# Two groups of the gMLP's down projection by Strassen's seven products, woven between its channel blocks

## The chip, the cores and the metric

The kernel runs on one core of one Trainium2 chip. The metric is the device time of one execution in microseconds (us), median over runs. The core has a matmul engine (PE, with its weight loads PEld), a vector engine (DVE), a scalar engine (ACT), GpSimd (POOL) and a sync engine (SP); each runs its own list of instructions in order, and they meet through semaphores. SP's list here is mostly weight loads from device memory; POOL's list holds some small operations and a few transfers.

## The reference, cut to what matters

Two layers, each FFN, mixer, FFN, gated embedding; the mixer of the first layer is an mLSTM, that of the second a gMLP. Everything is float32; x is 512 tokens by 1024 channels. The mixer in question:

```python
def gmlp_mixer(x, w_in, b_in, vn_g, vn_b, ws, bs, w_out):
    B, S, _ = x.shape
    NB = S // GM_BLOCK                                   # 4 blocks of 128 tokens
    u, v = jnp.split(jax.nn.gelu(x @ w_in + b_in, approximate=False), 2, axis=-1)   # 2048 channels each
    v = layer_norm(v, vn_g, vn_b).reshape(B, NB, GM_BLOCK, GM_GROUPS, GM_GDIM)
    blk = jnp.arange(GM_BLOCK) // CHUNK
    mask = blk[:, None] >= blk[None, :]
    ws_m = jnp.where(mask, ws, jnp.zeros((), ws.dtype))
    s = jnp.einsum('gts,bnsgc->bntgc', ws_m, v) + bs.T[:, :, None]
    return (u * s.reshape(B, S, GM_WIDTH)) @ w_out       # 512x2048 @ 2048x1024
```

The change is about the last line, the product with `w_out`.

## The kernel before, in words

**Precision.** Every float32 operand is split into a high and a low part (`split`: ACT makes the high part by a rounding copy, L273 for activations and L193 for weights; DVE subtracts it from the operand for the low part, L274 and L199). A product is then three matmuls, high by high, high by low, low by high: `mm3`, L268 to L270. For some weight tiles the low part is made by ACT and a DMA of POOL that adds the operand (L196, L197), which `release(low="dma")` asks for.

**Weights.** `Weights` holds one list (`order`) of all tiles of weights in the order in which they are used. A tile's raw operand comes from a load into one of three raw buffers (SP, L162); `fill` splits tiles into high and low ("main" buffers, four, and "extra" ones, two) as soon as `release` gives a buffer back, and each split frees, at its raw operand's last use, the raw buffer for the next load. So loads, ACT's and DVE's splits all follow from where `release` stands in the program. Loads go out in the order of the list.

**Strassen.** `Group` already does the FFNs' and the mLSTM's down projections by Strassen's seven products (Winograd's form) of two by two blocks: seven products where eight would do. Left factors come from `form` (additions on DVE, in place on the activations, then a split into `fhi`, `flo`), right factors from `Weights.forms` (additions on DVE, L105, L106, L110, L111, in place on the raw weights), products go to pinned PSUM banks `gps`, and `add` adds each product's bank to the residual `xt` (L591, L593).

**The gMLP.** After v has been normalised, the 2048 channels go by in 16 blocks of 128. In step b of the loop at the end of `gmlp`: `spatial(b)` is eight small matmuls into two banks `sps`, and DVE's five operations that make s from them (`gadd`, `gs`); `split_v(b+2)` splits the v of a later block (`gvh`, `gvl`, `gv`); `gate_u(b+1)` projects the next block's u with 24 matmuls into a bank `gups`, and ACT applies the Gelu (`guf`, L1280); `gated` multiplies s by u (L1315) and splits it into `hh`, `hl`; then one `release`. After the steps 3, 7, 11 and 15, `down` does four blocks at once: 96 matmuls into banks `dps`, added to `xt` by DVE. `up_bank` cycles over four PSUM banks, which `gups` and most `sps` share, so that a matmul into a bank waits for the bank's last reader: DVE's `gs` or ACT's `guf`.

Of the kernel before, what the change touches and what calls it, by code (L numbers as in the profile page):

```python
# [16 lines left out]
P = 128  # L17
# [3 lines left out]
TB = SEQ // P  # L21
# [216 lines left out]
def hybrid_trunk(ctx: ExitStack, tc, x, p, ln_g, ln_b, ffn1_wgu, ffn1_wd, ffn2_wgu, ffn2_wd,  # L238
# [9 lines left out]
    def stage_pool(name, bufs=1):  # L248
        return tc.tile_pool(name=name, bufs=bufs, side="left", reuse_waits="tile")
# [16 lines left out]
    def mm3(ps, st, mv, start, stop, more=False):  # L266

        mm(ps, st[0], mv[0], start=start, stop=False, skip_group_check=more)  # L268
        mm(ps, st[0], mv[1], start=False, stop=False, skip_group_check=more)  # L269
        mm(ps, st[1], mv[0], start=False, stop=stop, skip_group_check=more)  # L270
# [38 lines left out]
    def kp(w):  # L309
        return w.rearrange("(kb p) c -> p kb c", p=P)  # L310
# [56 lines left out]

    ML_SLOTS = (2, 3, 4, 5, 6, 7, 11)

    def stage_kinds(first):  # L370

        n = len(W.order) - first
        for i in range(n):
            extra = i % 6 >= 4 if i < n // 6 * 6 else i >= n - 2
            W.order[first + i] = ("extra" if extra else "main",) + W.order[first + i][1:]

    def ml_weights():
        win, wout = ml_w_in[0], ml_w_out[0]
        first = len(W.order)
        for h in range(HEADS):  # L380
            at = len(W.order)
            W.add((w_cols(win, h * DQK), cols2))
            W.add((w_cols(win, QK + h * DQK), cols2))
            add_wide(win, 2 * QK + h * DV)
            z0 = 2 * QK + INNER + h * DV
            W.add((w_cols(win, z0), cols2))
            W.add((w_cols(win, z0 + 2 * P), cols2))
            if h:
                tiles = W.order[at:]
                del W.order[at:]  # L390
                k = 4 * h - 4
                j0, j1 = W.add_load(kp(wout)[:, k:k + 2, :], 3), W.add_load(kp(wout)[:, k + 2:k + 4, :], 3, "gb")
                left, right = ((slice(None), slice(None), slice(c, c + 512)) for c in (0, 512))
                down_w = W.forms("", (j0, left), (j0, right), (j1, right), (j1, left))
                for i, tile_i in enumerate(tiles):
                    W.order.append(tile_i)
                    if i in ML_SLOTS:
                        W.order.append(down_w[ML_SLOTS.index(i)])
        add_rows(wout, 4 * HEADS - 4, 4)
        stage_kinds(first)  # L400
        for i, kind in zip(range(-4, 0), ("main", "extra", "extra", "main")):
            W.order[i] = (kind,) + W.order[i][1:]

    def gm_weights():
        win, wout = gm_w_in[0], gm_w_out[0]
        first = len(W.order)
        for c in range(4):
            add_wide(win, GW + c * 512)
        for b in range(16):
# [4 lines left out]
            if b and b % 4 == 0:  # L414
                add_rows(wout, b - 4, 4)
        add_rows(wout, 12, 4)
        stage_kinds(first)
# [312 lines left out]
    class Group:  # L730
# [2 lines left out]

        TO = ((0, 0), (0, 0), (0, 1), (1, 1), (1, 1), (0, 1), (1, 0))

        def __init__(self, h, pool, first=False):
            self.h, self.pool, self.half = h, pool, h.shape[1] // 2

            self.first = (0, 2, 3, 6) if first else ()
            self.ready, self.banks = deque(), []  # L740
            self.next_form = self.next_product = self.next_add = 0

        def form(self):

            def a(i, j):
                m = self.half
                return self.h[:, m * j - m:m * j, (i - 1) * 256:i * 256]
            a11, a12, a21, a22 = a(1, 1), a(1, 2), a(2, 1), a(2, 2)
            r = self.next_form
            if r == 7:  # L750
                return
            self.next_form += 1
            if r == 2:
                vec.tensor_add(a21, a21, a22)
                vec.tensor_sub(a11, a21, a11)  # L755
            elif r == 4:
                vec.tensor_sub(a21, a22, a11)
# [442 lines left out]


    def gmlp():
        with stage_pool("extra", EXTRA) as extra, stage_pool("gm_parts") as near, stage_pool("ghpool", 4) as hpool, \
                stage_pool("gm") as mp:
            W.open("extra", extra, EXTRA)
            vf = mp.tile([P, TB, GW], F32, name="gvf")

# [103 lines left out]
                    vs.append(split_v(b + 2))  # L1311
                return s

            def gated(s, uf):
                vec.tensor_mul(s, s, uf)  # L1315
                h = new_h(hpool)
                split(h[0], h[1], s)
                return h

            vs = deque([split_v(0), split_v(1)])  # L1320
            us, ss, hs = deque(), deque(), []
            for b in range(2):
                us.append(gate_u(b))
            for b in range(16):
                if b in (0, 14):
                    ss.extend(spatial(i, vs.popleft()) for i in (b, b + 1))
                    if b == 0:

                        W.refill(2)
                        W.release(2, low="dma")  # L1330
                elif b not in (1, 15):
                    ss.append(spatial(b, vs.popleft()))
                ahead = 0 < b < 15
                if ahead:
                    us.append(gate_u(b + 1))
                hs.append(gated(ss.popleft(), us.popleft()))
                if ahead and b < 14:
                    W.release(low="dma")
                elif b == 15:
                    W.release()  # L1340
                if b % 4 == 3:
                    down(hs, b == 3, Norm(1, 1) if b == 15 else None)
                    hs = []
            W.close("extra")

# [148 lines left out]
```

## Time and profile before

| | |
|---|---|
| median of 3 runs | 2232.38 us (2232.21 to 2232.38) |
| the profiled execution: its time, its span | 2232.51 us, 2230.8 us |
| PE, DVE, ACT busy, share of the span | 100%, 68%, 41% |
| PE's matmul rows in the program, before and with the change | 10173, 10149 |
| mean of one 128x512 matmul as listed | 389 ns |
| the gMLP's loop over blocks in this execution | about 1630 to 1812 us from the start |

In the profile each row names the line, the engine, the operation, what is written and read, and how often. Matmuls overlap in the array, so that the listed mean of one is its latency; the pace of a run of matmuls is read from the starts. Rows of waits give, for an engine, what ended its idle time, the sum, the count and the longest. The window view gives the busy time of each engine in a stretch of the span.

### The profile page before, as it was taken

Reading aid. Unit: us, or ns where it says so; the run is one execution under the profiler, and the core shown is the slowest. Engines: PE = TensorE matmul, PEld = TensorE weight load, DVE = VectorE, ACT = ScalarE, POOL = GpSimd, SP = SyncE. Lnnn points to the kernel's source line nnn. Section 1 sums busy time; section 2 is a strip of 40 time slices with the busy share of each in tenths; the row PEclk is TensorE's granted clock in tenths of the full one; section 3 lists DMA queues with packets and bytes.
Section 4 is the critical chain, followed back from the end, with each engine's and each line's share of the span. In section 5 each row is a group of like instructions: output and inputs, shape, how many; then the busy total and the mean of one; then the engine's idle time right before and its main releaser. Section 6 shows DMA issues by size and latency. Waiting matters only on the chain.

```text
span 2230.8 us, 26548 instructions
## 1 busy us (share of the span) xinstructions
PE 2220.3 (100%) x10589; PEld 1864.0 (84%) x10589; DVE 1526.0 (68%) x2240; ACT 913.9 (41%) x1298; POOL 101.8 (5%) x135
## 2 busy tenths in 40 slices
PE   9999999999999999999999999999999999999998
PEld 8888888888888888888889888888888888888887
DVE  5666667777776786666687666666666578666677
ACT  4333336454646533333255333334343453333332
POOL 1000000111101100000000000000010100000000
PEclk9999999999999999999999999999999999999999
DMA  7422323466847443332233422223355443332221
GB/s 231 130 93 88 95 85 100 100 149 135 166 107 161 123 139 126 95 104 67 95 123 122 133 86 87 93 87 109 106 142 142 104 151 123 122 113 85 85 85 57
DMA packets 202723, 253.56 MB, mean 114 GB/s; under 512 B 5812, under 2 KB 156468, under 8 KB 202600
## 3 DMA queue, kind: packets, MB, share of 16 engines
q1 hardware_dynamic: 168080, 211.83, 29.5%
q0 software_dynamic: 27904, 25.35, 7.9%
q10 hardware_dynamic: 6616, 14.69, 2.0%
q8 instruction: 83, 1.36, 0.2%
q14 instruction: 40, 0.33, 0.0%
HBM read 224.58 MB, written 2.11 MB: 102 GB/s over the span
## 4 chain that ended last, share of the span: by engine, by line
PE 99%; ACT 1%; DVE 0%; issue 0%; DVEq 0%; POOL 0%; POOLq 0%
PE fps L269 13%; PE fps L270 13%; PE fps L268 13%; PE gps L270 7%; PE gps L269 7%; PE gps L268 7%; PE dps L269 3%; PE dps L268 3%; PE dps L270 3%; PE gups L268 1%; PE vps L268 1%; PE zps L268 1%; PE zps L270 1%; PE vps L270 1%; PE gvps L268 1%; PE gups L269 1%
## 5 line engine op out<-in xcount | busy, mean ns | idle before, releaser
L268 PE MATMUL fps<-xh,whi 128*128 128x512 f32 x1312 | 510.7, 389 | 0.0
L269 PE MATMUL fps<-xl,whi 128*128 128x512 f32 x1312 | 510.5, 389 | 0.0
L270 PE MATMUL fps<-xh,wlo 128*128 128x512 f32 x1312 | 510.4, 389 | 0.0
L199 DVE TENSOR_TENSOR wlo<-wraw,whi 128x1024 fp32r<-128x1024 f32 (+1 forms) x286 | 345.4, 1218 | 149.5 <-ACT whi L193 147.8
L193 ACT ACTIVATE whi<-wraw 128x1024 fp32r<-128x1024 f32 (+1 forms) x334 | 346.5, 1048 | 185.8 <-PE fps L269 81.6
L199 DVE TENSOR_TENSOR wlo<-wquarter,whi 128x1024 fp32r<-128x1024 f32 (+1 forms) x140 | 156.5, 1118 | 218.2 <-ACT whi L193 218.2
L268 PEld LDWEIGHTS fps<-xh,whi 128*128 128x128 f32 x1312 | 246.3, 188 | 51.2
L269 PEld LDWEIGHTS fps<-xl,whi 128*128 128x128 f32 x1312 | 246.3, 188 | 51.1
L270 PEld LDWEIGHTS fps<-xh,wlo 128*128 128x128 f32 x1312 | 246.2, 188 | 51.0
L193 ACT ACTIVATE whi<-wquarter 128x1024 fp32r<-128x1024 f32 (+1 forms) x140 | 136.3, 974 | 279.8 <-PE gps L270 209.0
L270 PE MATMUL gps<-whi,flo 128*128 128x512 f32 x588 | 229.3, 390 | 0.0
L268 PE MATMUL gps<-whi,fhi 128*128 128x512 f32 x588 | 229.3, 390 | 0.0
L269 PE MATMUL gps<-wlo,fhi 128*128 128x512 f32 x588 | 229.2, 390 | 0.0
L593 DVE TENSOR_TENSOR xt<-xt,gps 128x512 f32<-128x512 f32 x282 | 180.3, 680 | 0.5 <-PE gps L270 0.5
L817 ACT ACTIVATE sg<-fps 128x512 f32<-128x512 f32 x80 | 47.9, 598 | 228.4 <-PE fps L270 228.4
L273 ACT ACTIVATE fhi<-h 128x512 fp32r<-128x512 f32 (+1 forms) x140 | 80.5, 581 | 142.9 <-DVE h L755 54.4
L269 PEld LDWEIGHTS gps<-wlo,fhi 128*128 128x128 f32 x588 | 110.4, 188 | 23.5
L268 PEld LDWEIGHTS gps<-whi,fhi 128*128 128x128 f32 x588 | 110.4, 188 | 23.3
L270 PEld LDWEIGHTS gps<-whi,flo 128*128 128x128 f32 x588 | 110.4, 188 | 23.3
L274 DVE TENSOR_TENSOR flo<-h,fhi 128x512 fp32r<-128x512 f32 (+1 forms) x140 | 87.2, 634 | 42.9 <-ACT fhi L273 42.9
L563 POOL TENSOR_TENSOR rs<-rs,eps_pow 128x1 f32<-128x1 f32 x32 | 20.6, 643 | 1556.4 <-DVE rs L562 1556.4
L466 ACT ACTIVATE xf<-xps,cols 128x128 f32<-128x128 f32 x160 | 59.8, 453 | 52.5 <-PE xps L461 52.5
(289 smaller groups left out, 3736.4 us busy)
## 6 DMA issues: line engine op xcount, KB each, us to landing
wraw<-in_ffn_wgu_dram SPq DMA_DIRECT2D x79, 1024.0 KB, 6.0
wquarter<-in_ffn_wd_dram SPq DMA_DIRECT2D x64, 512.0 KB, 3.7
wraw<-in_ml_w_in_dram SPq DMA_DIRECT2D x24, 1024.0 KB, 5.5
wlo<-wraw POOLq DMA_DIRECT2D x48, 512.0 KB, 6.5
wraw<-in_gm_w_in_dram SPq DMA_DIRECT2D x15, 1024.0 KB, 5.7
wraw<-in_ffn_wgu_dram SPq DMA_DIRECT2D x17, 512.0 KB, 4.0
wraw<-in_ffn_wd_dram SPq DMA_DIRECT2D x8, 1024.0 KB, 4.9
wraw<-in_ml_w_out_dram SPq DMA_DIRECT2D x8, 1024.0 KB, 4.9
```

Of the source, the lines that this page charges most:

```text
L193: self.nc.scalar.activation(hi[:, s], src[:, s], AF.Copy)
L199: self.nc.vector.tensor_sub(lo[:, s], src[:, s], hi[:, s].bitcast(F32))
L268: mm(ps, st[0], mv[0], start=start, stop=False, skip_group_check=more)
L269: mm(ps, st[0], mv[1], start=False, stop=False, skip_group_check=more)
L270: mm(ps, st[1], mv[0], start=False, stop=stop, skip_group_check=more)
L273: sca.activation(hi, src, AF.Copy)
L274: vec.tensor_sub(lo, src, hi.bitcast(F32))
L466: sca.activation(xf[:, k], ps[:, k], AF.Identity, scale=col("ln_g", norm.at + 4 * g + k), bias=col("ln_b", norm.at + 4 * g + k))
L563: pool.tensor_tensor(rs[:, 1:2], rs[:, 0:1], eps_pow, op=OP.pow)
L593: vec.tensor_add(dst, dst, ps)
L817: sca.activation(sg, ps, AF.Silu)
```

## The change: what it does

The blocks 0 to 3 and 4 to 7 are two groups; each goes down by `Group`'s seven products of 12 matmuls (84) in place of `down`'s 96. Blocks 8 to 15 still go by `down`, in two times four. The flag `by_tokens` only turns the layout of `Group`'s blocks. What moves with it:

- For blocks 0 to 7 the product s times u is written in place into `gvf` in float32, unsplit; DVE's additions of `form` work on it there, and each of seven factors is split, so the `hh`, `hl` of these blocks fall away.
- The table `GM_STEPS` says how many products stand behind each block: the first product behind block 3, one or two behind each until the last behind block 11. After each product DVE's addition of the product before last to `xt`, the next left factor (`form`), and then `release` follow.
- The two raw loads of a group's `w_out` (two rows of blocks each) and the seven right factors stand in `order` where their products come; eight DVE additions in all (four per group) are made in the raw weights, and the low parts of these seven tiles are made by DVE (L199) and not by ACT and POOL. A raw buffer that holds them is kept until the last factor.
- Loads of `gm_w_in` and `gm_w_out` alternate one by one in SP's list; before they went in pairs.
- `ghpool` has two buffers and not four; blocks 10, 11, 14 and 15 use the buffers of the left factors, and the splits of blocks 10 and 11 come behind the `release` of the weights.
- `stage_kinds` and `two_row_forms` are the rearranged code around it; the list of the mLSTM's weights stays the same.

```diff
+    GM_GROUPS = 2
+    GM_STEPS = {3: 1, 4: 1, 5: 2, 6: 2, 7: 2, 8: 1, 9: 2, 10: 2, 11: 1}
...
+    def two_row_forms(w, kind="raw"):
+        j0, j1 = W.add_load(w[:, :2], 3), W.add_load(w[:, 2:], 3, kind)
+        left, right = ((slice(None), slice(None), slice(c, c + 512)) for c in (0, 512))
+        return W.forms("", (j0, left), (j0, right), (j1, right), (j1, left))
...
+        down_w, k = deque(), 0
+        for b, tile_b in enumerate(tiles):
+            W.order.append(tile_b)
+            for _ in range(GM_STEPS.get(b - 1, 0)):
+                if not down_w:
+                    down_w.extend(two_row_forms(kp(wout)[:, k:k + 4, :]))
+                    k += 4
+                W.order.append(down_w.popleft())
+            if b % 4 == 0 and b > 4 * GM_GROUPS:
+                assert not down_w
                 add_rows(wout, b - 4, 4)
...
                 for k in range(self.half):
-                    mm3(ps, [a[:, k, e * P:(e + 1) * P] for a in f], [a[:, k] for a in w],
+                    i, j = (e, k) if self.by_tokens else (k, e)
+                    mm3(ps, [a[:, i, j * P:(j + 1) * P] for a in f], [a[:, k] for a in w],
                         k == 0 and r in (0, 1, 3), k == self.half - 1, r not in (0, 1, 3))
...
-            def gated(s, uf):
+            def gated(b, s, uf):
+                if b < 4 * GM_GROUPS:
+                    dst = vf[:, :, b * P:(b + 1) * P]
+                    vec.tensor_mul(dst, s.rearrange("p (t c) -> p t c", t=TB), uf.rearrange("p (t c) -> p t c", t=TB))
+                    return
                 vec.tensor_mul(s, s, uf)
...
             for b in range(16):
+                add()
...
-                hs.append(gated(ss.popleft(), us.popleft()))
-                if ahead and b < 14:
+                s = gated(b, ss.popleft(), us.popleft())
+                late = b >= 4 * GM_GROUPS and b % 4 >= 2 and b in GM_STEPS
+                if b >= 4 * GM_GROUPS and not late:
+                    split_gated(b, s)
+                if b in (2, 3):
+                    form()
+                for i in range(GM_STEPS.get(b, 0)):
+                    add()
+                    products.popleft().product()
+                    form()
+                    W.release(1 if i + 1 < GM_STEPS[b] else 2, low="dma")
+                if late:
+                    split_gated(b, s)
```

**Where instructions move: DVE at the start of the loop.** DVE's list in step 0, before: the low parts of two weight tiles, then the first gated products with their splits.

```order
L274 TENSOR_TENSOR gv<-gvf,gv 128x512
L199 TENSOR_TENSOR wlo<-wraw,whi 128x1024 x2
L1315 TENSOR_TENSOR gs<-gs,guf 128x512
L274 TENSOR_TENSOR hl<-gs,hh 128x512
L1315 TENSOR_TENSOR gs<-gs,guf 128x512
```

With the change (`wraw_12751` holds u weights, `wraw_12810` the first and `wraw_13042` the second half of the first group's `w_out`):

```order
L199 TENSOR_TENSOR wlo_13039<-wraw_12751,whi_13038 128x1024
L199 TENSOR_TENSOR wlo_13045<-wraw_12810,whi_13044 128x1024
L199 TENSOR_TENSOR wlo_13054<-wraw_13042,whi_13053 128x1024
L1344 TENSOR_TENSOR gvf_12285<-gs_13008,guf_12967 128x4x128
L1344 TENSOR_TENSOR gvf_12285<-gs_13029,guf_12994 128x4x128
L1329 SCALAR_TENSOR_TENSOR gadd_13103<-rsum_12616,cols_108 128x128
```

A third low part, of the tile that comes from `wraw_13042`, now stands ahead of the first gated products; that load is the one that reuses the buffer of `wraw_12751`.

**ACT between the Gelus of blocks 4 and 5.** Before, with `guf_13205` the Gelu of block 4 and `guf_13397` that of block 5 (the four whole tiles belong to `down` behind block 3):

```order
L1280 ACTIVATE guf_13205<-gups_13180,cols_108 128x512
L273 ACTIVATE hh_13208<-gs_13171 128x512
L193 ACTIVATE whi_13212<-wraw_13039 128x1024
L196 ACTIVATE wlo_13213<-wraw_13039 128x1024
L193 ACTIVATE whi_13311<-wraw_13050 128x1024
L193 ACTIVATE whi_13321<-wraw_13050 128x1024
L193 ACTIVATE whi_13333<-wraw_13099 128x1024
L193 ACTIVATE whi_13343<-wraw_13099 128x1024
L273 ACTIVATE gvh_13368<-gvf_12282 128x512
L1280 ACTIVATE guf_13397<-gups_13372,cols_108 128x512
```

With the change `guf_13198` is block 4's and `guf_13284` block 5's:

```order
L1306 ACTIVATE guf_13198<-gups_13173,cols_108 128x512
L273 ACTIVATE fhi_13201<-gvf_12285 128x512
L273 ACTIVATE fhi_13221<-gvf_12285 128x512
L193 ACTIVATE whi_13227<-wraw_12810 128x1024
L193 ACTIVATE whi_13231<-wraw_13091 128x1024
L196 ACTIVATE wlo_13232<-wraw_13091 128x1024
L273 ACTIVATE gvh_13255<-gvf_12285 128x512
L1306 ACTIVATE guf_13284<-gups_13259,cols_108 128x512
```

`whi_13227` reads the weights that DVE's L111 has just written in place, `fhi_13221` the activations that its L780 has written; both stand ahead of block 5's Gelu. The second bank of block 5's `sps` is the bank `gups_13259`.

**DVE behind block 7**, where the last product of the first group and the first of the second stand together; all of it is new there, in this order:

```order
L274 TENSOR_TENSOR flo<-gvf,fhi 128x512
L105 TENSOR_TENSOR wraw<-wraw 128x2x512
L106 TENSOR_TENSOR wraw<-wraw 128x2x512
L199 TENSOR_TENSOR wlo<-wraw,whi 128x1024
L613 SCALAR_TENSOR_TENSOR xt<-xt,gps 128x512 x2
L779 TENSOR_TENSOR gvf<-gvf 128x2x256
L780 TENSOR_TENSOR gvf<-gvf 128x2x256
L274 TENSOR_TENSOR flo<-gvf,fhi 128x512
L110 TENSOR_TENSOR wraw<-wraw 128x2x512
L111 TENSOR_TENSOR wraw<-wraw 128x2x512
L199 TENSOR_TENSOR wlo<-wraw,whi 128x1024
L615 TENSOR_TENSOR xt<-xt,gps 128x512 x2
```

Both pairs of weight additions of the second group and two left factors now come between the gated product of block 7 and the `gadd` of block 8; before, DVE had only the additions of `down`'s banks and low parts of weights there.

More of the change, by code (lines that the diff above doesn't have):

```diff
@@ L408, in gm_weights @@
             add_wide(win, GW + c * 512)
+        at = len(W.order)
         for b in range(16):
@@ L1312, in spatial, with split_gated, form, add @@
                 return s
-            def gated(s, uf):
-                vec.tensor_mul(s, s, uf)
-                h = new_h(hpool)
-                split(h[0], h[1], s)
-                return h
+            def gated(b, s, uf):
[3 more added lines that the diff above has]
+                    return
+                vec.tensor_mul(s, s, uf)
+                return s
+            def split_gated(b, s):
+                if b % 4 < 2:
+                    h = new_h(hpool)
+                else:
+                    h = [fpool.tile([P, 2, 256], F32R, name=n, tag=n).rearrange("p t c -> p (t c)") for n in ("fhi", "flo")]
+                split(h[0], h[1], s)
+                hs.append(h)
+            groups = [Group(vf[:, :, g * 512:(g + 1) * 512], fpool, g == 0, True) for g in range(GM_GROUPS)]
+            forms, products, added = (deque(g for g in groups for _ in range(7)) for _ in range(3))
+            def form():
+                if forms:
+                    forms.popleft().form()
+            def add():
+                if len(added) > len(products):
+                    added.popleft().add()
             vs = deque([split_v(0), split_v(1)])
```

29 lines of the change are left out of this document (16 added, 13 removed).

## The prediction

> **What bounds the kernel now.** First I read the page's busy time with its chain of waits, then PE's waits by releaser.
>
> ```profile
> PE 2220.3 (100%) x10589; PEld 1864.0 (84%) x10589; DVE 1526.0 (68%) x2240; ACT 913.9 (41%) x1298; POOL 101.8 (5%) x135
> PE 99%; ACT 1%; DVE 0%; issue 0%; DVEq 0%; POOL 0%; POOLq 0%
> PE warm L1447 <- POOL ident masks.py:199: 1.4, 1, 1.4
> PE sup L696 <- DVE wlo L199: 0.2, 1, 0.2
> PE sup L696 <- ACT whi L193: 0.2, 1, 0.2
> ```
>
> PE sets the end by itself: in 2230.8 us it waits three times, 1.8 us in all, at the start. So whatever PE is spared comes off the time, and whatever wait is put on it goes on in full. Next, windows of the gMLP loop (busy us and count of each engine), one of the mLSTM behind them for comparison:
>
> ```profile
> 1672.00:1720.00 48.00, 48.00 (x229) 40.30 (x228) 26.82 (x45) 19.57 (x25) 4.84 (x4) 1.00 0.57 132
> 1720.00:1767.00 47.00, 47.00 (x225) 39.45 (x224) 26.02 (x44) 18.56 (x24) 4.83 (x4) 1.00 0.57 123
> 530.00:630.00 100.00, 100.00 (x489) 84.30 (x488) 71.55 (x141) 52.66 (x76) 14.46 (x17) 1.00 0.63 137
> ```
>
> The columns are PE, PEld, DVE, ACT, POOL, the granted clock, DMA share and GB/s. In the gMLP DVE is busy 56% of PE's time (26.82 of 48.00), so there is room; the mLSTM, which already weaves such products in, has DVE at 72% and PE without a wait.
>
> **What is removed: 24 matmuls.** PE's timeline, start and latency:
>
> ```profile
> 1639.60 0.28 PE L1300 MATMUL sps<-wsp,gvh 128*128 128x256 f32 x1
> 1640.47 0.45 PE L268 MATMUL gups<-xh,whi 128*128 128x512 f32 x1
> 1645.98 0.28 PE L1300 MATMUL sps<-wsp,gv 128*128 128x256 f32 x1
> 1646.85 0.45 PE L268 MATMUL gups<-xh,whi 128*128 128x512 f32 x1
> ```
>
> 24 matmuls take 1645.98 - 1640.47 = 5.51 us, 0.23 each (the listed 389 ns is latency); eight `sps` take 0.87; a block step without products is 6.38. A product of 12 is then 2.75 us, and a group spares 12 of them. **Gain: 24 x 0.23 = 5.5 us.** The 24 matmuls are removed where PE is the only bound, so this is certain.
>
> **What is added on DVE.** Groups of DVE's instructions in the loop, and the two kinds of additions as the mLSTM and FFN have them:
>
> ```profile
> L199 DVE TENSOR_TENSOR wlo<-wraw,whi 128x1024 fp32r<-128x1024 f32 x15 | 18.3, 1224 | 6.9 <-ACT whi L193 6.0
> L593 DVE TENSOR_TENSOR xt<-xt,dps 128x512 f32<-128x512 f32 x22 | 14.8, 683 | 22.1 <-PE dps L270 22.1
> L1309 DVE SCALAR_TENSOR_TENSOR gs<-sps,cols,gs 128x256 f32<-128x256 f32 x28 | 13.6, 484 | 1.0
> L1307 DVE SCALAR_TENSOR_TENSOR gs<-sps,cols,gadd 128x256 f32<-128x256 f32 x28 | 13.4, 479 | 1.5
> L274 DVE TENSOR_TENSOR hl<-gs,hh 128x512 fp32r<-128x512 f32 x16 | 11.1, 693 | 22.3 <-ACT hh L273 22.3
> L1315 DVE TENSOR_TENSOR gs<-gs,guf 128x512 f32<-128x512 f32 x16 | 11.0, 685 | 0.0
> L1303 DVE SCALAR_TENSOR_TENSOR gadd<-rsum,cols 128x128 f32<-128x128 f32 x14 | 4.8, 345 | 0.0
> L274 DVE TENSOR_TENSOR gvl<-gvf,gvh 128x512 fp32r<-128x512 f32 x6 | 4.1, 681 | 0.0
> L105 DVE TENSOR_TENSOR wraw<-wraw x3: 1218/1219/1220, 464.9 to 660.5; 128x1024 f32<-128x1024 f32 x3
> L111 DVE TENSOR_TENSOR wraw<-wraw x3: 1226/1227/1227, 474.5 to 670.0; 128x1024 f32<-128x1024 f32 x3
> L757 DVE TENSOR_TENSOR h<-h x20: 418/684/685, 58.3 to 2106.2; 128x512 f32<-128x512 f32 x16, 128x256 f32<-128x256 f32 x4
> ```
>
> For one group of four blocks: 14 additions to `xt` at 0.68 (9.6), four additions of left factors at 0.68 (2.7), seven low parts `flo` at 0.69 (4.9), four additions of weights at 1.22 (4.9), seven `wlo` at 1.22 (8.6), and four times a block's own 0.35 + 4 x 0.48 + 0.68 + 0.69 = 3.64 (14.6): **45.3 us**. PE needs 4 x 6.38 + 7 x 2.75 = **44.8 us** for it. DVE goes from 56% to 101% before it waits for anything. And it does wait:
>
> ```profile
> DVE hl L274 <- ACT hh L273: 22.3, 16, 2.2
> DVE wlo L199 <- ACT whi L193: 6.0, 6, 1.8
> ACT whi L193 <- DVE wraw L111: 7.3, 2, 3.7
> L193 ACT ACTIVATE whi<-wraw 128x1024 fp32r<-128x1024 f32 x27 | 28.5, 1054 | 46.6 <-PE dps L270 46.6
> L196 ACT ACTIVATE wlo<-wraw 128x1024 fp32r<-128x1024 f32 x14 | 14.6, 1045 | 0.0
> L1280 ACT ACTIVATE guf<-gups,cols 128x512 f32<-128x512 f32 x14 | 9.6, 687 | 38.9 <-PE gups L270 38.9
> ```
>
> Each split that follows its operand at once holds DVE some 0.7 us for a `fhi` or `hh` and 1.1 for a `whi`: 7 x 0.7 + 2 x 1.1 = 7 us a group. The products do stretch over nine blocks, so that single steps are lighter; what decides is the order in which ACT and DVE stand in each other's way.
>
> **The first stall.** DVE's and SP's timelines where the loop begins, and the landing times (shortest, median, longest) of SP's loads in the loop, the page's lines of both kinds of load and of POOL's transfers, and two neighbours of ACT's timeline:
>
> ```profile
> 1638.22 2.35 DVE L199 TENSOR_TENSOR wlo<-wraw,whi 128x1024 fp32r<-128x1024 f32 x2
> 1640.49 0.68 DVE L1315 TENSOR_TENSOR gs<-gs,guf 128x512 f32<-128x512 f32 x1
> 1639.46 6.46 SPq L162 DMA_DIRECT2D wraw<-in_gm_w_in_dram  x2
> wraw<-in_gm_w_out_dram SPq DMA_DIRECT2D x8, 1024.0 KB, 4.9
> DMA to landing us min/median/max: 3.7/5.0/9.9
> wraw<-in_gm_w_in_dram SPq DMA_DIRECT2D x15, 1024.0 KB, 5.7
> wlo<-wraw POOLq DMA_DIRECT2D x48, 512.0 KB, 6.5
> 1648.61 1.05 ACT L193 ACTIVATE whi<-wraw 128x1024 fp32r<-128x1024 f32 x1
> 1649.56 1.04 ACT L196 ACTIVATE wlo<-wraw 128x1024 fp32r<-128x1024 f32 x1
> ```
>
> The load that goes out at 1639.46, when the first of those two `wlo` frees its buffer, is with the change the second half of `w_out`. By the median it lands at 1644.4; DVE's third `wlo`, which now stands ahead of the gated products, starts at 1645.5 behind its `whi`. DVE, free at 1640.6 before, has lost 4.9 us. From there I add the rows in DVE's order: third `wlo` and two gated products to 1648.0; block 2's `gadd`, `gs`, `gvl`, gated product 1651.5; `flo` of the first product 1652.1 (PE asks for it at 1652.4: in time); L105, L106 1654.6; `wlo` behind its `whi` 1656.9; block 3 and its gated product 1660.4; `flo` 1661.7; L779, L780 and the next `flo` 1664.4; L110, L111 **1666.8**. ACT, whose next in line is the `whi` of these weights, then does `whi`, `whi`, `wlo`, `gvh`, `guf`; neighbours start 0.95 apart where one is listed at 1.05, so these five take 4.2 from there: block 5's Gelu ends at **1671.0**. PE, without a wait until there, has block 4's projection from 1646.85, a product, `sps`, block 5's projection and a product behind it: 1646.85 + 5.51 + 2.75 + 0.87 + 5.51 + 2.75 + 0.44 = 1664.7, when it needs the bank that this Gelu reads. **Stall 6.4 us**; everything behind it in PE's queue waits along. With the load landing at 3.7 it is 5.2, at 9.9 it is 11.4; if two of DVE's waits for ACT are hidden by work in between, 4. Another 0.4 follows at block 6's projection, whose bank DVE's `gs` of block 4 still reads.
>
> **The second stall.** From 1671.5 PE goes on to block 9. The weights of block 9's u come from a load that waits for its buffer until POOL's transfer of block 8's low part, which ACT's `wlo` lets out near 1685, has landed 6.5 later; the load lands 5.7 after that, at 1697.5, and ACT's `whi` of it, first in its queue, holds the next `fhi` and block 8's Gelu. DVE then has a `flo`, a `wlo`, two additions, block 7's `gadd` and `gs`, `gv` and gated product, 1700.2 to 1706.5 by the rows above. Behind block 7 1.4 (`flo`), 2.4 (L105, L106), 2.3 (`wlo` behind `whi`), 1.3 (additions), 1.3 (L779, L780), 1.4 (`flo`) and 2.4 (L110, L111) follow on each other in ACT's and DVE's queues, with a wait of about 1 for a product among them: L111 ends near 1720, block 9's Gelu five instructions later at **1724.2**. PE, at two products a step, is there at 1717.2, after 1.0 of waiting for DVE's addition to a product's bank. **Stall 7.0 + 1.0**, 0.4 behind it; 4.6 with transfers as short as the shortest, 12 with one of 9.9.
>
> **Behind it.** For blocks 8 to 11 I come to 2.6 us of waits (the last products' additions 2.0, the late splits of block 11 0.6). That far down, gaps of DVE may have absorbed them: between 0 and 2.6 I take the middle, 1.3.
>
> **Free of cost:** the in-place gated product has L1315's size; fewer transfers by POOL only lighten its queue; two `hh` buffers are enough because blocks 0 to 7 use none, and if not, the wait would stand with the third term.
>
> **Sum:** 6.4 + 0.4 + 1.0 + 7.0 + 0.4 + 1.3 - 5.5 = +11.0 us. Against the profiled execution's 2232.5: 2243.5; the median of the runs is 0.1 lower, so **2243.4 us**. Its own bounds: 4.0 + 4.6 - 5.5 = +3.1 (2235.5) up to, say, one transfer at 9.9: +5 (2248.5).
>
> **Rivals.**
>
> *The clock falls in the stalls.* The row that speaks for it stands at the very start, where PE came from idleness:
>
> ```profile
> 1.43 3.67 PE L1447 MATMUL warm<-ident 128*128 128x128 f32 x16 [1.43 <-POOL ident masks.py:199]
> 7.64 1.25 PE L1447 MATMUL warm<-ident 128*128 128x128 f32 x10
> ```
>
> The same matmul takes 0.23 us at first and 0.125 after, so 16 of them lost 3.67 - 16 x 0.125 = 1.67 us, although the granted clock reads 1.00 in every window. If a stall of 6 us puts PE back into that state, both cost 1.7 more: 2246.8. Against it: no row shows PE idle for more than 1.4 us later on. [...]
>
> *The stalls are hidden.* What decides is ACT's place: if block 5's Gelu ended by 1664.7, 6.4 us earlier than I have it, nothing would wait. For it: in the mLSTM L111 holds ACT 3.7 us at a time and PE never waits; DVE's lateness starts with one load, and the splits may overlap better than one behind the other. Then only the gain is left: 2232.4 - 5.5 = 2226.9, **faster**. Against it: 101% of DVE's time.
>
> *One stall alone.* If the early load lands soon and DVE catches up in the light steps, one stall of about 5 to 7 eats the gain: 2232 to 2234, the same.
>
> **How the numbers follow.** Forecast 0.50, clock rival 0.20, hidden 0.17, one stall 0.13. Over 0.2% (4.5 us, about what a measurement of this kernel can tell) lies all of the first two but the forecast's lowest end: slower 0.70; same 0.13; faster 0.17. The likeliest's own range is 2235.5 to 2248.5. The range reaches up to 2250 for the clock rival and down to 2226.5 to take in the hidden case, since leaving that out would leave out 0.17 and the upper tail.
>
> **What would show it.** PE's waits name `sps <- ACT guf` twice, near 1664 and 1717, of 4 to 8 us; DVE above 90% between 1645 and 1720; DVE's third `wlo` idle some 5 us for ACT's `whi`; the load of `w_out` issued at 1639.5. PE's matmuls 24 fewer at 0.23. I am wrong if PE waits for under 5.5 us in the loop, or if it waits for weights (`gups <- POOL wlo`) and not for banks.

## The result: 0.75% slower, from two stalls and what follows them

| | before | after |
|---|---|---|
| median | 2232.35 us (2232.21 to 2232.38, 4 runs) | 2249.07 us (2248.78 to 2249.48, 4 runs) |
| profiled execution: time, span | 2232.51, 2230.8 us | 2248.95, 2247.2 us |

The ratio is 1.0075, 95% interval 1.0058 to 1.0093: +16.7 us, where +11.0 was forecast. The page of the changed kernel, busy time and the chain that ended last:

```profile
PE 2221.3 (99%) x10565; PEld 1862.5 (83%) x10565; DVE 1555.4 (69%) x2279; ACT 923.9 (41%) x1311; POOL 105.7 (5%) x136
...
PE 95%; DVE 2%; ACT 1%; DMA 1%; issue 1%; SPq 0%; DVEq 0%; ACTq 0%; POOLq 0%
```

24 matmuls fewer (10565 are listed, 10589 before), and yet PE is listed as busy 1.0 us longer, in a span 16.4 us longer. The chain now runs 5% of the way through other engines, where it was 1%. PE's waits by releaser (sum, times, longest):

```profile
PE sps L1326 <- ACT guf L1306: 12.4, 2, 6.3
...
PE dps L268 <- DVE xt L615: 1.2, 1, 1.2
PE dps L268 <- ACT fhi L273: 0.7, 1, 0.7
```

Two waits for the bank that a Gelu reads, and two short ones at the end of the woven stretch: 14.3 us. Where they lie, and what else happens there, the windows of 10 us show (PE, PEld, DVE, ACT, POOL, granted clock, DMA share, GB/s):

```profile
1650.00:1660.00 10.00, 10.00 (x49) 8.26 (x48) 8.63 (x15) 2.64 (x4) 0.71 (x1) 1.00 0.77 144
1660.00:1670.00 10.00, 5.63 (x25) 4.02 (x23) 7.33 (x9) 3.47 (x5) 0.00 (x0) 0.94 0.04 13
1670.00:1680.00 10.00, 8.11 (x30) 6.79 (x31) 9.68 (x18) 4.95 (x8) 1.54 (x1) 0.72 0.69 129
...
1710.00:1720.00 10.00, 8.39 (x40) 6.86 (x38) 7.99 (x10) 1.69 (x2) 0.00 (x0) 1.00 0.39 112
1720.00:1730.00 10.00, 5.47 (x15) 4.51 (x16) 7.82 (x14) 6.57 (x9) 1.54 (x1) 0.67 0.47 52
```

PE loses 4.37 + 1.89 us in the first place and 1.61 + 4.53 in the second. But where it is busy again, it does less: from 1670 to 1680 it gets 30 matmuls done in 8.11 us, where 49 go into a full window. The granted clock there is 0.72, behind the second stall 0.67, and 1.00 in the windows where nothing waits. PE's timeline behind the first stall shows the pace:

```profile
1671.89 0.58 PE L1326 MATMUL sps<-wsp,gv 128*128 128x256 f32 x1 [6.26 <-ACT guf L1306]
...
1672.83 0.77 PE L268 MATMUL gups<-xh,whi 128*128 128x512 f32 x1
...
1674.67 0.63 PE L269 MATMUL gups<-xl,whi 128*128 128x512 f32 x1
1675.10 0.60 PE L270 MATMUL gups<-xh,wlo 128*128 128x512 f32 x1
1675.53 0.40 PE L268 MATMUL gups<-xh,whi 128*128 128x512 f32 x1
1675.77 0.39 PE L269 MATMUL gups<-xl,whi 128*128 128x512 f32 x1
```

Matmuls of one shape start 0.43 us apart until 1675.5 and 0.23 apart from there. Behind the second stall (it ends at 1724.53, after 6.14 us) the slow pace lasts until 1730.2. By the starts, against 0.23 for a matmul, the slow ones lose 1.7 and 2.7 us.

Now the chain of events that was forecast for the first stall, from SP's, ACT's and DVE's timelines of the changed kernel:

```profile
1639.51 0.37 SPq L162 DMA_DIRECT2D wraw<-in_gm_w_out_dram  x1
...
1645.34 1.06 ACT L193 ACTIVATE whi<-wraw 128x1024 fp32r<-128x1024 f32 x1 [6.63 <-DMA wraw<-in_gm_w_out_dram]
1646.43 1.23 DVE L199 TENSOR_TENSOR wlo<-wraw,whi 128x1024 fp32r<-128x1024 f32 x1 [5.82 <-ACT whi L193]
...
1666.53 1.23 DVE L111 TENSOR_TENSOR wraw<-wraw 128x1024 f32<-128x1024 f32 x1
1667.79 2.00 ACT L193 ACTIVATE whi<-wraw 128x1024 fp32r<-128x1024 f32 x2 [3.15 <-DVE wraw L111]
...
1671.17 0.67 ACT L1306 ACTIVATE guf<-gups,cols 128x512 f32<-128x512 f32 x1
```

The load takes 5.8 us to land, ACT waits 6.63 for it, DVE stands 5.82 before the third `wlo`, and the lateness reaches L111, ACT's `whi` and block 5's Gelu, which ends at 1671.84. PE had been at the bank since about 1665.6. Three rows from the path to the second stall:

```profile
1698.31 1.06 ACT L193 ACTIVATE whi<-wraw 128x1024 fp32r<-128x1024 f32 x1 [3.48 <-DMA wraw<-in_gm_w_in_dram]
...
1719.18 1.22 DVE L111 TENSOR_TENSOR wraw<-wraw 128x1024 f32<-128x1024 f32 x1
...
1723.82 0.67 ACT L1306 ACTIVATE guf<-gups,cols 128x512 f32<-128x512 f32 x1
```

Here too ACT waits for a load, that of block 9's weights, before the row of work behind block 7 begins.

**The balance, by the starts of matmuls.** The stalls 6.42 + 6.30, the slow matmuls behind them 1.7 + 2.7, the two late waits with the slower first matmuls behind each 2.7, six gaps of 0.11 to 0.16 between matmuls around 1647 and 1662 (not explained) 0.7, together 20.5; less 5.5 of gain, 15.0. The last matmul starts at 2237.54 and not at 2222.07: 15.47 later. So all but 0.5 us is found in the loop. The other 0.9 of the span lies behind the last matmul (9.7 us from its start to the end, 8.7 before): the engines' rows there are as before, but the last store of the output takes 3.0 us to land, where no store took more than 2.1 before. In nine of the ten experiments below this tail is 8.7, in one (the low part in between, alone) 9.8, with a last store of 3.1. Why a store takes longer is not shown.

### The profile page after: what moved, and what is told of

Read it like the earlier page. It is cut to its first block, busy times and chain, and to the rows that moved or that the text cites. A ratio compares the mean times of both kernels' runs of the same rounds, so it can differ in the third digit from the quotient of the medians.

```text
span 2247.2 us, 26579 instructions
## 1 busy us (share of the span) xinstructions
PE 2221.3 (99%) x10565; PEld 1862.5 (83%) x10565; DVE 1555.4 (69%) x2279; ACT 923.9 (41%) x1311; POOL 105.7 (5%) x136
## 4 chain that ended last, share of the span: by engine, by line
PE 95%; DVE 2%; ACT 1%; DMA 1%; issue 1%; SPq 0%; DVEq 0%; ACTq 0%; POOLq 0%
PE fps L269 13%; PE fps L268 13%; PE fps L270 13%; PE gps L268 7%; PE gps L269 7%; PE gps L270 7%; PE dps L270 2%; PE dps L268 2%; PE dps L269 2%; PE vps L268 1%; PE zps L268 1%; PE zps L270 1%; PE vps L270 1%; PE gvps L270 1%; PE gvps L268 1%; PE zps L269 1%
## 5 line engine op out<-in xcount | busy, mean ns | idle before, releaser
L199 DVE TENSOR_TENSOR wlo<-wraw,whi 128x1024 fp32r<-128x1024 f32 (+1 forms) x291 | 351.1, 1218 | 157.1 <-ACT whi L193 155.1
L193 ACT ACTIVATE whi<-wraw 128x1024 fp32r<-128x1024 f32 (+1 forms) x340 | 352.1, 1048 | 184.5 <-PE fps L269 81.6
L199 DVE TENSOR_TENSOR wlo<-wquarter,whi 128x1024 fp32r<-128x1024 f32 (+1 forms) x140 | 156.5, 1118 | 218.4 <-ACT whi L193 218.4
L270 PE MATMUL gps<-whi,flo 128*128 128x512 f32 x644 | 251.3, 390 | 0.0
L268 PE MATMUL gps<-whi,fhi 128*128 128x512 f32 x644 | 251.2, 390 | 0.0
L269 PE MATMUL gps<-wlo,fhi 128*128 128x512 f32 x644 | 251.0, 390 | 0.0
L615 DVE TENSOR_TENSOR xt<-xt,gps 128x512 f32<-128x512 f32 x302 | 192.9, 679 | 0.5 <-PE gps L270 0.5
L270 PEld LDWEIGHTS gps<-whi,flo 128*128 128x128 f32 x644 | 120.9, 188 | 26.2 <-DVE flo L274 0.6
L268 PEld LDWEIGHTS gps<-whi,fhi 128*128 128x128 f32 x644 | 120.9, 188 | 25.7 <-ACT fhi L273 0.3
L269 PEld LDWEIGHTS gps<-wlo,fhi 128*128 128x128 f32 x644 | 120.9, 188 | 25.6
```

What stands on the lines that cost most here:

```text
L193: self.nc.scalar.activation(hi[:, s], src[:, s], AF.Copy)
L199: self.nc.vector.tensor_sub(lo[:, s], src[:, s], hi[:, s].bitcast(F32))
L615: vec.tensor_add(dst, dst, ps)
```

## The experiments

**The second group's weight additions left out.** The forecast laid the second stall on what stands in a row behind block 7. Here the four additions of weights of the second group are left out, so that its products use weights that were not combined; this part of the output is not computed.

```diff
-    def two_row_forms(w, kind="raw"):
+    def two_row_forms(w, kind="raw", adds=True):
...
-                    down_w.extend(two_row_forms(kp(wout)[:, k:k + 4, :]))
+                    down_w.extend(two_row_forms(kp(wout)[:, k:k + 4, :], adds=k == 0))
```

> Leaves out the four DVE additions in the second group's weights (L105, L106, L110, L111), so that its products use unformed weights; nothing else changes. DVE does 4.9 us less, all of it behind block 7. Theory A (the chain additions, whi, Gelu behind block 7 makes the second stall): the second stall of 6.1 us falls below 1.5, its slow matmuls (2.7 us) go too, the first stays at 6.3: 2249.1 - 5 - 2.7 - 1 = about 2240 (2239 to 2242). Rival (the late load of block 9's weights makes it): the second stall stays over 4 us, 2246 to 2249. Theory B (total work): 4.9 us less at most, without the clock's part if the wait stays over 3 us: 2244.

Measured: 2242.16 us, ratio 1.0042 (1.0027 to 1.0057). PE's waits for the Gelu:

```profile
PE sps L1328 <- ACT guf L1308: 7.3, 2, 6.3
```

The first stall is unchanged (6.28), the second is 1.06 and no slow matmuls follow it. Four DVE instructions of 1.22 us, 4.9 us in all, took 5.1 us of the stall with them: they do lie on the path to block 9's Gelu, one for one. The time is just above A's range. That does not clear the late load of block 9's weights, the rival in the expectation: its wait comes earlier on the path that the forecast traced, so that both may belong to it, and no run takes that load away.

**Two products behind block 3.** One product more behind block 3 and one fewer behind block 6. The list of loads moves with it: the load of `w_out`'s second half now stands one place earlier.

```diff
-    GM_STEPS = {3: 1, 4: 1, 5: 2, 6: 2, 7: 2, 8: 1, 9: 2, 10: 2, 11: 1}
+    GM_STEPS = {3: 2, 4: 1, 5: 2, 6: 1, 7: 2, 8: 1, 9: 2, 10: 2, 11: 1}
```

> One line of the table: two products behind block 3, one behind block 6 (3:2, 6:1). The second half of the first group's w_out then goes out one place earlier in SP's list. Theory A (the two stalls are two places, the first one made by that load: DVE idle 5.8 us, Gelu of block 5 late): the first stall of 6.3 us and the slow matmuls behind it go, some 2 us of waiting for a left factor at the second product take their place; the second stall stays at 4 to 6: 2249.1 - 8.2 + 2 = about 2243 (2241 to 2245). Theory B (DVE's total work is the bound, 101% of PE's time, and waits move about): within 2 us of 2249.

Measured: 2243.41 us, ratio 1.0049 (1.0032 to 1.0065).

DVE's timeline at the start of the loop has its three low parts in one piece now:

```profile
1637.85 3.49 DVE L199 TENSOR_TENSOR wlo<-wraw,whi 128x1024 fp32r<-128x1024 f32 x3
```

PE's waits:

```profile
PE sps L1326 <- ACT guf L1306: 5.6, 2, 4.2
PE dps L268 <- DVE xt L615: 2.8, 1, 2.8
PE gps L268 <- ACT fhi L273: 1.6, 1, 1.6
```

With the load earlier, DVE does not stand still ahead of its third low part, and the first stall is gone; in its place there are short waits (1.56 and two of about 0.6). The waits that come later remain: 1.31 and 4.24 for Gelus, 2.81 for an addition to `xt`. The time is in A's range. But the run moves a product too, so it does not show the load's part alone. L111 ends at 1663.61, 4.15 earlier; block 5's Gelu, with one more `whi` and an `fhi` ahead of it, ends at 1669.16, 2.7 earlier. PE, with 2.75 us more of products ahead and the short waits, comes to the bank only at about 1670.4, 4.8 later, and that alone would have taken most of the stall.

**The second group spread out.** One product behind block 7 and two behind block 11, so that the row of work behind block 7 is shorter.

```diff
-    GM_STEPS = {3: 1, 4: 1, 5: 2, 6: 2, 7: 2, 8: 1, 9: 2, 10: 2, 11: 1}
+    GM_STEPS = {3: 1, 4: 1, 5: 2, 6: 2, 7: 1, 8: 1, 9: 2, 10: 2, 11: 2}
```

> The table again: one product behind block 7 and two behind block 11 (7:1, 11:2), so that the second group starts one block later and its weights' additions do not all stand behind block 7. Theory A, if the crowd behind block 7 alone made the second stall: it falls under 1 us and nothing takes its place, 2249.1 - 8 = about 2241. Theory B (DVE has no room in blocks 3 to 11, whatever the order): products of the second group now wait for DVE's additions to their banks, 0.5 to 4 us each, 7 to 9 us in all in blocks 8 to 11; with fewer long stalls a little less is lost to the clock: 2246 to 2250.

Measured: 2250.16 us, ratio 1.0078 (1.0063 to 1.0093): no better, and about what B expected.

```profile
PE sps L1326 <- ACT guf L1306: 6.3, 1, 6.3
PE gps L268 <- DVE xt L615: 5.7, 2, 3.8
PE sps L1326 <- DVE gs L1335: 1.9, 1, 1.9
```

The Gelu of block 9 is in time, and PE waits 1.92 for a `gs`, 3.76 and 1.91 for additions to the products' banks instead: the waits move to other results of DVE, and each of the four pauses is followed by slow matmuls.

**One group.** Blocks 4 to 7 go down by the 96 matmuls again.

```diff
-    GM_GROUPS = 2
-    GM_STEPS = {3: 1, 4: 1, 5: 2, 6: 2, 7: 2, 8: 1, 9: 2, 10: 2, 11: 1}
+    GM_GROUPS = 1
+    GM_STEPS = {3: 1, 4: 1, 5: 2, 6: 2, 7: 1}
```

> The change with one group of four blocks (0 to 3) by seven products; blocks 4 to 7 go by the 96 matmuls again. Theory A, that each group brings its own gain and its own stall: 12 matmuls fewer (-2.75 us), the first stall as it was (6.3 listed, about 2 of slow matmuls behind it), about 0.5 of small waits: about 2238.5 (2237 to 2240), slower than before, PE's waits with one sps <- ACT guf and none near 1724. Theory B, that the two groups' work on DVE and ACT adds up until block 9: the first stall becomes smaller too and the time comes to 2230 to 2234.

Measured: 2244.75 us, ratio 1.0058 (1.0044 to 1.0072). The wait is where A had it, with nothing near 1724:

```profile
PE sps L1326 <- ACT guf L1306: 6.3, 1, 6.3
...
PE dps L268 <- DVE xt L615: 0.9, 1, 0.9
```

So the first group makes its stall by itself, which speaks against B. But the time is 6 us above A's: by the starts, `down` of blocks 4 to 7 comes with waits of 2.6, a later `down` with 1.6, the slow matmuls behind the stall with 2.9 (they last until 1678.5). Half of the change brings three quarters of the slowdown, 12.4 of 16.7 us.

**Pauses put into the kernel before.** To see the slow matmuls without the change, blocks 3, 6, 10 and 13 of the kernel before get extra copies on ACT behind their Gelus, and PE a transposition that waits for the last of them.

```diff
+                fillers = {3: 3, 6: 5, 10: 7, 13: 10}.get(b, 0)
+                for _ in range(fillers):
+                    sca.activation(uf, ps, AF.Copy)
+                if fillers:
+                    nc.tensor.transpose(dn_bank("held")[:, :P], uf[:, :P], ident)
```

> The kernel before, with four pauses of PE put in by ACT: behind the projections of u of blocks 3, 6, 10 and 13 ACT copies the bank 3, 5, 7 and 10 times, and a small transpose on PE waits for the last copy. Pauses of about 2.3, 3.7, 5.2 and 7.3 us, 18.5 in all. If a pause of 6 us halves the matmul pace for a while whatever the kernel (clock theory), matmuls behind the longer pauses start 0.43 us apart for 3 to 5 us and those behind the shortest stay at 0.23: 2232.4 + 18.5 + 2 or 3 x 2 = 2255 to 2258. If the slow matmuls of the changed kernel come from something else there (DVE or transfers at the same time), all stay at 0.23: 2251.

Measured: 2258.12 us (one run). The pauses came to 1.95, 3.20, 4.46 and 6.34 us, and each was followed by slow matmuls, the shortest too, which had been expected to pass:

```profile
PE held L1284 <- ACT guf L1282: 15.9, 4, 6.3
```

PE's timeline behind the first of them:

```profile
1648.01 0.33 PE L1284 MATMUL held<-ident,guf 128*128 128x128 f32 x1 [1.95 <-ACT guf L1282]
...
1651.10 0.63 PE L269 MATMUL gups<-xl,whi 128*128 128x512 f32 x1
1651.52 0.63 PE L270 MATMUL gups<-xh,wlo 128*128 128x512 f32 x1
...
1652.29 0.39 PE L269 MATMUL gups<-xl,whi 128*128 128x512 f32 x1
```

The `gups` matmuls behind them lost 1.4, 1.9, 1.8 and 0.7 us: the loss does not grow with the pause. So such a pause, here of 1.95 us and more, is enough for the slow pace; nothing else of the change is needed.

**The order of the two engines' lists.** The next runs leave all the added work in and change where it stands (in all but the first, two low parts of weights also go from ACT and POOL to DVE). In the first, a left factor's low part no longer follows its `fhi` on DVE at once but comes between ACT's `whi` and DVE's `wlo` of the weights, so that neither waits for the other's latest. (The first two lines stand in `fill` behind ACT's `whi`.)

```diff
+                if between:
+                    between.popleft()() if len(between) else None
...
-                    form()
-                    W.release(1 if i + 1 < GM_STEPS[b] else 2, low="dma")
+                    low_part = deque()
+                    form(low_part)
+                    W.release(1 if i + 1 < GM_STEPS[b] else 2, low="dma", between=low_part)
+                    while low_part:
+                        low_part.popleft()()
```

> The changed kernel with one edit only: the low part of a left factor between ACT's whi and DVE's wlo. It spares DVE some 0.7 to 1.4 us at each of the four places where weights are formed. Theory A: the first stall falls from 6.3 to about 5, the second from 6.1 to 3, the down product's wait rises to 2: 2249.1 - 1.3 - 3 + 0.5 = about 2245 (2242 to 2246), since all three are long enough for the clock. Theory B: 1 to 2 us less, 2247.

Measured: 2244.6 us, ratio 1.0055 (1.0039 to 1.007). It is in A's range. Both Gelus are late still; the stalls shrink to 4.81 and 3.03, and slow matmuls follow both. So this place of one instruction made 4.6 us of the stalls' 12.4.

**Three other edits, without that one.** One product fewer behind block 6 (`6: 1` in the table), one product ahead of block 5's projection; 1, 2 and 1 weight buffers given back in steps 0, 1 and 2 in place of 2, 1 and 1, by which the loads go out otherwise; two low parts of weights, behind blocks 4 and 10, by DVE, and the splits of blocks 10 and 11 not behind the `release`.

```diff
+                if b == 4:
+                    add()
+                    products.popleft().product()
+                    form()
+                    W.release(1, low="dma")
...
-                    W.release(low="dma")
+                    W.release({1: 2, 2: 1}.get(b, 1), low="dma")
```

> As the one with all four edits, without the low part between. Theory A: the stall behind block 7 is back at 4.3 us with slow matmuls behind it (2 us), and a product waits 1.5 for DVE: 2232.4 - 5.5 + 6.5 + 2 = about 2235.5 (2234 to 2238). Theory B: as the changed kernel but for the first stall, 2241 or more.

Measured: 2237.67 us, ratio 1.0022 (1.0013 to 1.0031).

```profile
PE sps L1326 <- ACT guf L1306: 4.2, 1, 4.2
...
PE gps L268 <- DVE xt L613: 1.4, 1, 1.4
```

This is in A's range. The first stall is gone, the second is 4.24 with six slow matmuls of `gups` behind it.

**Both together.** The product ahead of block 5's projection now hands its low part on as well.

```diff
-                    form()
-                    W.release(1, low="dma")
+                    low_pre = deque()
+                    form(low_pre)
+                    W.release(1, low="dma", between=low_pre)
+                    while low_pre:
+                        low_pre.popleft()()
```

> Both groups stay, with the same 24 matmuls less. Four edits: one product (the first group's second) goes ahead of block 5's projection and one is taken from block 6; the releases at the loop's start are dealt out 1, 2, 1; the low part of a left factor (DVE) stands between ACT's whi and DVE's wlo of the weights released with it, so that DVE waits for neither; blocks 10 and 11 are split at once, and the weights released after the first product behind block 4 and the last behind block 10 have their low parts made by DVE. Theory A (the stalls are made by the order of the queues): every wait that I find by going along the rows is under 0.6 us, 2.2 in all, too short for the clock: 2232.4 - 5.5 + 2.2 = about 2229 (2228 to 2232), faster than before. Theory B (DVE's total work, which is the same): it cannot get under 2236.

Measured: 2233.31 us (11 runs), ratio 1.0003 (0.9994 to 1.0012).

```profile
PE sps L1333 <- ACT guf L1313: 1.3, 1, 1.3
```

The window over blocks 7 to 11 (PE, PEld, DVE, ACT, POOL, clock, DMA share, GB/s):

```profile
1690.00:1750.00 60.00, 58.15 (x273) 47.87 (x272) 51.56 (x82) 28.91 (x38) 6.39 (x5) 1.00 0.62 124
```

Neither number was met, but the mechanism was: no pause over 1.3 us, no slow matmul, a clock of 1.00, and DVE busy 51.56 of 60 us (86%) while PE loses less than 2. What is left are six waits of 3.2 us as listed. By the starts they take 5.4, since each costs another 0.2 to 0.6 until the matmuls flow again; that is all of the gain.

**The same with two products behind block 3** in place of the product ahead of the projection.

```diff
-    GM_STEPS = {3: 1, 4: 1, 5: 2, 6: 1, 7: 2, 8: 1, 9: 2, 10: 2, 11: 1}
+    GM_STEPS = {3: 2, 4: 1, 5: 2, 6: 1, 7: 2, 8: 1, 9: 2, 10: 2, 11: 1}
```

> As the one with all four edits, but the first group's second product stands behind block 3 and not ahead of block 5's projection. Theory A: the product then waits 1.4 to 1.7 us for its left factor, 2.3 in all: 2229.2, and 2231 if that wait is already long enough for slow matmuls behind it. Theory B: over 2236.

Measured: 2233.89 us (11 runs), ratio 1.0005 (0.9996 to 1.0014). Its longest wait is 1.54, for an `fhi` early in the loop, where it was 1.26 for a Gelu; the six listed waits come to 3.7 in place of 3.2, and the median is 0.6 longer, less than the spread of the runs. This number, too, lies between A's and B's.

**Block 2's s made while DVE waits.** All of the above, and in step 1 DVE makes block 2's `gadd` and `gs` between two low parts of weights, where it waited 2.7 us for ACT. (Its expectation calls the buffers given back one earlier; it is the 1, 2, 1 of above, one later in step 0. It puts the listed waits of the run with both edits at 2.6 us; they are the 3.2 above.)

```diff
+                    if b == 1:
+                        between.extend([lambda: None, lambda: ss.append(spatial(2, vs.popleft()))])
+                    W.release({1: 2, 2: 1}.get(b, 1), low="dma", between=between)
```

> The kernel with all four edits of the earlier run (low part of a left factor between ACT's whi and DVE's wlo, buffers given back one earlier, one product ahead of block 5's projection, single steps) and one more: in step 1, DVE makes block 2's s (gadd, gs) between two low parts of weights, in the time in which it waits for ACT. Theory A, that only the order of ACT's and DVE's lists takes the gain and that the waits left in that run (2.6 us as listed, 5.5 by the starts) came from DVE reaching the first products late: most of them go, PE waits under 0.5 us each and 1 to 2.5 in all by the starts, no slow matmuls, 2228.5 to 2230.5 us, faster than before. Theory B, that DVE's and ACT's added work sets the pace and waits only change place: 2232.5 to 2234, no better than that run.

Measured: 2231.33 us (2231.07 to 2231.88, 11 runs) against 2232.40 (2232.06 to 2232.93, 15 runs) of the kernel before beside it; ratio 0.9996 (0.9987 to 1.0005).

```profile
PE sps L1333 <- ACT guf L1313: 1.0, 1, 1.0
PE dps L270 <- DVE xt L617: 0.5, 1, 0.5
...
PE dps L270 <- ACT fhi L275: 0.5, 1, 0.5
```

The waits at the first products are gone, as A had it, and the ones from block 9 on are not: 2.3 us as listed, 3.8 by the starts. The median is 1.1 us below the kernel before and no run of one reaches into the other's, but the interval of the ratio holds 1. It lies between A and B, and nearer to A: the work fits on DVE and ACT; the waits that are left, and what they cost beyond their length, still take most of the gain.

## Why the prediction was right in sign and place, and short by 5.7 us

| term | forecast | measured, by starts |
|---|---|---|
| 24 matmuls | -5.5 | -5.5 |
| first stall | 6.4 | 6.4 |
| second stall | 7.0 | 6.3 |
| waits around them (0.4, 1.0, 0.4) | 1.8 | none |
| behind block 9 | 1.3 | 2.7 |
| slow matmuls after the stalls | rival: 3.4 | 4.4 |
| small gaps before the first stall | - | 0.7 |
| behind the last matmul, the last store | - | 0.9 |
| not placed | - | 0.5 |
| sum | +11.0 | +16.4 (span) |

The measured time lies above the forecast's own range (2235.5 to 2248.5), and below 2250 only because that end had been set for the clock.

- **The gain** held: 24 matmuls fewer, and the others 0.23 apart by the starts where the granted clock is 1.00 and PE does not wait.
- **The first stall** is right by mechanism, place and size. Single steps were each about 0.9 late: the load needs 5.8 and not 4.9, the third `wlo` starts at 1646.43 (1645.5), L111 ends at 1667.76 (1666.8), the Gelu at 1671.84 (1671.0). PE is late by as much (1665.6 for 1664.7), mostly from small gaps that were not in the sum, so that the difference stays: that the two errors cancel is luck. That the load is at its root is read from the chain of waits; the run with the load moved ahead moved a product as well, and no run moves the load alone.
- **The second stall** was traced through a dozen steps to L111 "near 1720" and a Gelu that ends at 1724.2; L111 ends at 1720.40 and the Gelu at 1724.49. PE came at about 1718.2, not 1717.2, so the stall is 0.7 shorter. The load on the way there was as forecast: ACT has block 9's weights at 1698.3, for 1697.5. Without the four additions 5.1 us of it go.
- **"DVE goes to 101%"** did not show as such. In the 75 us from 1645 to 1720 it is busy 59.65 us:

```profile
1645.00:1720.00 75.00, 67.13 (x310) 55.37 (x308) 59.65 (x91) 32.00 (x42) 7.71 (x5) 0.95 0.57 111
```

  That is 80%, against the "above 90%" of the signs. The kernel with both edits has 94.61 us in the 110 from 1640 to 1750 (86%) and hardly waits there. So what decided was the order, as the sentence behind the 101% said, and not the amount of work; the 45.3 us for a group spread over nine blocks were a poor bound for a stretch.
- **The failed step is the clock**, which stood among the rivals at 0.20 and "against it: no row shows PE idle for more than 1.4 us later on". That was no evidence against it; the trace of before had no pause in which it could have shown. The start's row (16 matmuls at 0.23 and then 0.125) was the better guide: 1.7 us a stall by it, 1.7 and 2.7 measured.
- **Small waits** were put in the wrong places: none at blocks 6 and 10, none for a product's bank, and 2.7 at the first `dps` of blocks 8 to 11 where 1.3 was taken as the middle between 0 and 2.6.
- **Hidden** and **one stall alone** are refuted for this order of work. With another order the second of them comes true in kind (the run with three edits, one stall, but 2237.7 and not 2232 to 2234), and the first in part (no wait over 1.1 us, but 2231.3 and not 2226.9): both rested on DVE and ACT having the time, which they have.

## What to carry to other kernels

When PE sets the end, count what a saving adds to the engines in front of PE not only as work but as a sequence: here 5.5 us of matmuls were saved for a gain of about 1 even in the best order found. In the changed kernel each `whi` of a weight that DVE has just combined stands ahead of a Gelu whose bank PE needs. Price every forecast pause of PE of about 2 us or more with slow matmuls behind it: here they followed all 17 pauses of 1.91 us or more in the loop, and 0.7 to 2.9 us were measured for them, 1.7 and 2.7 behind the two stalls. And a load that the change moves in its queue has to be followed to the engine that stands first in line for it: DVE stood 5.82 us behind one such load, ahead of a stall of 6.26.

## What the runs showed of the hardware that was not expected

**Pauses of 1.91 us were already followed by slow matmuls.** In the loop of the changed kernel and of the ten experiments all 17 pauses of PE of 1.91 us or more were. The shortest of them are 1.91, 1.92 and 1.95 us, the longest pauses that were not followed by slow matmuls 1.54, 1.55, 1.56 and 1.59. From PE's timeline of the spread-out second group:

```profile
1709.43 0.36 PE L1326 MATMUL sps<-wsp,gvh 128*128 128x256 f32 x1 [1.92 <-DVE gs L1335]
```

The `gups` matmuls behind it start 0.43 apart from 1710.25 to 1713.24. From that of the low part in between:

```profile
1756.14 0.50 PE L270 MATMUL dps<-whi,hh 128*128 128x512 f32 x1 [1.59 <-DVE xt L617]
1756.48 0.39 PE L271 MATMUL dps<-wlo,hh 128*128 128x512 f32 x1
1756.71 0.40 PE L272 MATMUL dps<-whi,hl 128*128 128x512 f32 x1
```

Here they start 0.23 apart from the second on.

**A slow stretch need not begin with the pause's end.** In the run with the low part in between, PE's timeline behind the stall of 3.03 us:

```profile
1721.61 0.40 PE L270 MATMUL gups<-xh,whi 128*128 128x512 f32 x1
1721.84 0.57 PE L271 MATMUL gups<-xl,whi 128*128 128x512 f32 x1
```

PE has worked at its full pace since 1719.89, with one wait of 0.27, when it turns slow at about 1721.9; it is fast again at 1725.3, 3.4 later. The granted clock says the same. Three windows of this length, the last over the slow stretch (PE, granted clock, DMA share, GB/s):

```profile
1715.07:1718.48 3.41, 1.79 (x11) 1.00 0.00 0
1718.48:1721.89 3.41, 1.72 (x9) 1.00 0.23 26
1721.90:1725.30 3.40, 3.40 (x10) 0.50 1.15 128
```

The pause of 3.03 us lies in the first two of these windows: the clock stays at 1.00 through it and for 2.0 us behind it (1719.89 to 1721.89), and is 0.50 in the third. In the changed kernel the clock is at 0.50 for 6.8 us with each stall, about twice as long as here (columns as in the windows of 10 us):

```profile
1668.70:1675.53 6.83, 3.64 (x11) 3.06 (x11) 6.46 (x12) 6.07 (x9) 1.54 (x1) 0.50 0.43 48
...
1723.32:1730.14 6.82, 5.61 (x15) 4.65 (x16) 5.76 (x12) 3.83 (x7) 1.54 (x1) 0.50 0.69 77
```

Of the first 3.2 us passed while PE still waited, of the second 1.2; PE worked 3.64 and 5.61 us at the low clock. That is the difference between 1.7 and 2.7 us after two stalls of one length.

In these executions the ends of the slow stretches lie close to whole multiples of 3.41 us (half of the 6.83 above) apart: in the changed kernel, by the granted clock, 1675.53 and 1730.14 (54.61, 16.0 times), with the pauses in the kernel before, by the starts of the matmuls, about 1652.2, 1700.0, 1754.6 and 1802.3 (14.0, 16.0 and 14.0 times). No run shows what sets these lengths, nor why pauses of 1.91 us were followed by slow matmuls and those of 1.59 us were not.

**Waits cost more than their listed length here.** The stall listed at 6.26 is 6.42 by the starts, one of 1.21 with what follows 1.48, and in the best order 2.3 us of listed waits take 3.8, in the run with both edits 3.2 take 5.4. For these two sums of short waits that is more than half on top.
